# A transformer trunk on one core: x fetched in halves, the root spread later, the memory tokens later

## The chip, the core and the metric

The kernel runs on one core of a Trainium2 chip. Its engines work side by side and wait for each other through semaphores: PE (TensorE, matrix products and transposes), PEld (PE's weight loads), DVE (VectorE), ACT (ScalarE), POOL (GpSimd) and SP (SyncE, which here only issues transfers). The metric is the device time of one execution in microseconds, median of several runs. A difference of less than about 0.3% (1.1 us here) can't be told from no change, since three runs of one kernel lie that far apart.

## The reference, cut to what matters

One layer on x of 256 tokens and 1024 features, all in float32: a mixer of four attention groups of four heads (dilated, stick-breaking, sliding window, block-sparse), a cross-attention into 256 memory tokens, and a squared-ReLU MLP, each with a residual, then a last RMSNorm.

```python
for l in range(DEPTH):
    x = x + hybrid_mixer(rmsnorm(x, g_mix[l]), w_in[l], g_group[l], sinks[l], w_out[l], rel_table)
    x = x + memory_cross_attention(rmsnorm(x, g_cross[l]), rmsnorm(mem, g_mem[l]),
                                   w_xq[l], w_xkv[l], w_xo[l])
    x = x + squared_relu_mlp(rmsnorm(x, g_mlp[l]), w_up[l], w_down[l])
return rmsnorm(x, g_final)
```

## The kernel before, in words

**The products.** Tokens are handled in two blocks of 128 rows, t = 0 and 1. A float32 product is made of three products of float32r parts (high with high, high with low, low with high), `mm3`. So each operand is split: ACT writes the high part (`w<-raw` on L313, `hThi<-tmp` on L396), DVE the rest as the low part (`w<-raw,w` on L314, `hTlo<-tmp,hThi` on L397). Weights come in halves of 512 KB (tile `raw`, four buffers, issued by SP on L299): a fifth half can be issued only when the first half's low part is made.

**The head of the program.** Both blocks of x are fetched (L328), their sums of squares taken on ACT (`sq<-x`, L388), and they are transposed on PE (L403), multiplied by the gain on DVE (`tmp<-ps,gT`, L413) and split into hT. The gain itself is transposed on PE (L374) and copied by ACT (`gT<-ps`, L375). Warm-up products of zeros (`warm`, L365) fill PE before. Then come the projections of the first group: av (48 products on L491), aq and ak (48 each on L420 to L422), then bq and bk. I write av0, av1 and so on for the halves of a weight unit.

**The reciprocal root.** DVE makes the variance (L382), POOL raises it to the power -0.5 (`rstd`, L383), PE transposes the two results (L455, "spread"), ACT copies them to `rk` and `rq` (L458, L459), and DVE multiplies q and k by them when their products are complete (L506).

**The bias.** PE makes a strip by distance (L467), DVE adds its mask (`k<-ps,k`, L468), POOL writes it to DRAM (`dstrip`, L469) and fetches it back in Toeplitz layout, 512 KB for each of three groups and 128 KB for one (L709), on POOL's own queue.

**What sets the order.** Operations are recorded with what they read and write and a price. `Plan.arrange` is a list schedule over the engines: of the operations that can start when an engine gets free, it takes the one with the longest way to the end. Each engine then runs its instructions strictly in that order, so that a wait of one holds up all behind it on its engine. A `raw` or `w` buffer is taken in the order of the recording.

Of the kernel before, what the change touches and what calls it, by code (L numbers as in the profile page):

```python
# [18 lines left out]
P = 128  # L19
S = 256  # L20
D = 1024
# [21 lines left out]
def _constants():  # L43
    """One-hot of minus the bucket of each distance, and the additive mask of each bias row.
    Column u stands for the distance u - 127. Rows 0-3 dilated, 4-7 window, 8-11 causal, 12 strictly past."""
# [17 lines left out]
class Buf:  # L63
    """A tile that is taken from its pool when the first operation on it is issued."""
# [21 lines left out]
class Plan:  # L86
    """Records operations with what they read and write, and issues them in the order of a list schedule:
    of the operations that can start when an engine gets free, the one with the longest way to the end."""
# [126 lines left out]
def trunk(ctx: ExitStack, tc: tile.TileContext, a: dict, out: bass.AP):  # L215
# [24 lines left out]
    def copy(n, out_, in_, r, w):  # L240
        """A copy out of PSUM, by whichever engine is free first."""
        plan.add("DVE", 0.065 + n * 1.05e-3, lambda: nc.vector.tensor_copy(out_(), in_()), r, w,
                 ("ACT", 0.02 + n * 0.00093, lambda: nc.scalar.activation(out_(), in_(), AF.Copy)))
# [10 lines left out]
    def dma_late(nbytes, fn, r, w):  # L254
        """On the queue of GpSimd."""
        plan.add("POOL", 1.0, fn, r, w)
        plan.add("DMA", max(0.06, nbytes / 360e3), None, [], w)
# [34 lines left out]
    def load(u, *which):  # L292
        """Fetches and splits halves of a unit."""
# [23 lines left out]
    def wt(u, k):  # L317
        """Row block k of a unit: the two buffers and the block's place in them."""
        got, n = parts[u]
        return got[k // n], k % n  # L320

# [5 lines left out]
    def load_x(t):  # L327
        dma(P * D * 4, lambda: nc.sync.dma_start(xt[t].t, a["x"][0, tsl(t), :]), [], [xt[t]])  # L328
# [9 lines left out]
    load_x(0)  # L338
    load_gain(0, nc.scalar)
    load("av", 0)  # L340
    load_x(1)
    load("av", 1)
    ident, mhalf, warm = buf("ident", [P, P]), buf("mhalf", [P, 1]), buf("warm", [P, 512], BF16)
    pool(0.5, lambda: make_identity(nc, ident.t), [], [ident])
    pool(0.05, lambda: nc.gpsimd.memset(mhalf.t, -0.5), [], [mhalf])
    dve(512, lambda: nc.vector.memset(warm.t, 0.0), [], [warm])
# [13 lines left out]
    def warm_up(n):  # L360
        """Products of nothing, so that the array's clock is up when the first ones come."""
        wps = acct()
        plan.fixed = -1.0
        for _ in range(n):
            pe(0.11, lambda: nc.tensor.matmul(wps[:, 0:P], warm[:, 0:P], warm[:, 0:P], start=True, stop=True), [warm], [wps])  # L365
# [5 lines left out]
    def gains_T(i):  # L371
        n = grow[i].shape[0]
        gps = pst()
# [6 lines left out]
    def rstd_of(ssq, n):  # L380
        v, r = buf("var", [P, 1], F32, 4), buf("rstd", [P, 1], F32, 16)
        dve(1, lambda: nc.vector.tensor_scalar(v.t, ssq.t, 1.0 / n, EPS, op0=ALU.mult, op1=ALU.add), [ssq], [v])  # L382
        pool(0.5, lambda: nc.gpsimd.tensor_tensor(r.t, v.t, mhalf.t, op=ALU.pow), [v, mhalf], [r])  # L383
        return r

    def rstd_row(src, view, n):
        sq, ssq = buf("sq", [P, D], BF16, 1), buf("ssq", [P, 1], F32, 4)
        act(n, lambda: nc.scalar.activation(sq[:, 0:n], view(), AF.Square, accum_out=ssq.t), [src], [sq, ssq], 1)  # L388
        return rstd_of(ssq, n)
# [9 lines left out]
    def transpose(dst, src, view, n, keys):  # L399
        """n blocks of 128 columns of view(), transposed side by side into dst."""  # L400
# [5 lines left out]
    def gained_T(x, g, hl, t):  # L406
        """The transposed rows of x, times the gain, split: (t, half of the blocks) at a time."""
# [21 lines left out]
    def proj_T(dst, view, u, i, hT):  # L429
        """view()[c, t] = sum_k w[k, c] hT[k, t]"""  # L430
# [5 lines left out]
    def proj(dst, view, u, hT, t):  # L436
        """view()[t, c] = sum_k hT[k, t] w[k, c]"""
# [6 lines left out]
    h1 = pair("hT", KB, 2)  # L444
    r1 = []
    for t in range(2):
        gained_T(xt[t], 0, h1, t)
        r1.append(rstd_row(xt[t], lambda t=t: xt[t].t, D))
# [77 lines left out]
    def transpose_probs(w, t):  # L526
        """w [t, 4, s] -> per head the blocks [s, t], each with its buffer."""
# [15 lines left out]
    def weigh(pT, v, kv, vkeys):  # L543
        """Weighted values and their sums: [t, 4, 65]."""
# [26 lines left out]
    # ---- scores of 128 queries and 256 keys by float32r products: a head's two parts of k above each other in the  # L571
    #      rows of the array, met by the high part of q twice; then the low part of q with the high part of k ----
# [3 lines left out]
    def stack_k(k, view, n):  # L576
        """Slot 2 i + half: the high part of the head's rows, and in the other rows their low part."""
# [8 lines left out]
    def stack_q(q, view):  # L586
        """The high part twice, above each other, and the low part in its own rows."""
# [107 lines left out]
    def rows_mm(acc, hl, u, t, c0, c1, first, last):  # L695
        """acc += columns c0 to c1 of the sum over the two row blocks of a unit"""
# [19 lines left out]
    for gi in range(4):  # L716
# [3 lines left out]
        if gi == 1:  # L720
            mem = [buf("tmp", [P, D], F32, 3) for _ in range(2)]
            for t in range(2):
                dma(P * D * 4, lambda t=t: nc.sync.dma_start(mem[t].t, a["mem"][0, tsl(t), :]), [], [mem[t]])
# [93 lines left out]
    def up_rows(i, hid, t):  # L817
        """Two blocks of hidden features for one block of tokens alone."""
# [107 lines left out]
```

## Time and profile before

| | |
|---|---|
| median of 3 runs | 361.29 us (360.21 to 361.37) |
| span of the profiled execution, first to last instruction | 357.2 us |
| median less span (launch and end, outside the span) | 4.1 us |
| PE busy | 347.0 us, 97% of the span |
| DVE, ACT, POOL busy | 230.7, 194.1, 24.9 us |
| DMA | 59.88 MB, 168 GB/s over the span |

The time of the profiled execution is known by its span alone; sums are made against 357.2 us, and the 4.1 us around it are taken as constant. PE's busy time counts a product until its modelled end, so 97% says that PE rarely has nothing in flight, not that it is at its peak.

### The profile page before, as it was taken

The page shows a single profiled execution, that of the slowest core. Times are in us where ns is not written, and L with a number is a line of the kernel's source. Part 1 is how long each engine was busy: PE and PEld are TensorE (multiplying, and loading weights), DVE is VectorE, ACT ScalarE, POOL GpSimd, SP SyncE. Part 2 cuts the span into 40 slices and gives each one's busy share as a digit, 9 for nine tenths or more (in the row PEclk, how much of TensorE's full clock was granted, in tenths as well). Part 3 has the DMA queues.
Part 4 walks back from the last instruction along what each step waited for, and adds up shares of the span by engine and source line. Part 5 has one row for each costly group of instructions (what it writes and reads, how often), then busy time and mean ns, then how long its engine had stood idle before and what let it go on. Part 6 is the DMA issues. An engine that isn't in the chain of part 4 may idle for free.

```text
span 357.2 us, 6139 instructions
## 1 busy us (share of the span) xinstructions
PE 347.0 (97%) x2442; PEld 316.9 (89%) x2442; DVE 230.7 (65%) x370; ACT 194.1 (54%) x313; POOL 24.9 (7%) x44
## 2 busy tenths in 40 slices
PE   7899999999999999999999999999999999999992
PEld 6798999989888889878999999999999999999982
DVE  3857779579886699668946445464555545465254
ACT  6577677377873467684654435354353534535132
POOL 5430100000201005000010000000000000000000
PEclk9999999999999999999999999999999999999998
DMA  8998574640245335825375555655466554653003
GB/s 247 357 348 254 140 217 124 229 119 0 65 167 182 120 118 159 260 65 167 103 252 178 176 163 192 219 181 192 137 218 195 185 200 135 229 190 107 2 0 117
DMA packets 39900, 59.88 MB, mean 168 GB/s; under 512 B 2006, under 2 KB 33040, under 8 KB 39872
## 3 DMA queue, kind: packets, MB, share of 16 engines
q1 hardware_dynamic: 39216, 57.69, 50.3%
q0 software_dynamic: 640, 1.80, 1.7%
q8 instruction: 19, 0.31, 0.3%
q14 instruction: 9, 0.07, 0.1%
q10 hardware_dynamic: 16, 0.00, 0.0%
HBM read 58.42 MB, written 1.07 MB: 167 GB/s over the span
## 4 chain that ended last, share of the span: by engine, by line
PE 91%; DVE 2%; issue 2%; DMA 2%; POOL 1%; ACT 0%; SPq 0%; POOLq 0%; DVEq 0%
PE acc L420 15%; PE acc L421 15%; PE acc L422 15%; PE ps L421 11%; PE ps L420 11%; PE ps L422 11%; PE ps L553 4%; PE ps L403 3%; PE ps L601 2%; PE ps L600 2%; PE ps L535 2%; DMA x<-in_x_dram 2%; POOL rstd L383 1%; PE ps L629 1%; DVE hTlo L397 1%
## 5 line engine op out<-in xcount | busy, mean ns | idle before, releaser
L314 DVE TENSOR_TENSOR w<-raw,w 128x1024 fp32r<-128x1024 f32 x100 | 120.3, 1220 | 83.4 <-ACT w L313 80.0
L313 ACT ACTIVATE w<-raw 128x1024 fp32r<-128x1024 f32 x100 | 103.4, 1054 | 93.7 <-PE ps L421 43.5
L421 PE MATMUL ps<-hTlo,w 128*128 128x256 f32 x256 | 72.2, 282 | 0.0
L420 PE MATMUL ps<-hThi,w 128*128 128x256 f32 x256 | 72.0, 281 | 0.0
L422 PE MATMUL ps<-hThi,w 128*128 128x256 f32 x256 | 71.8, 280 | 0.0
L420 PE MATMUL acc<-w,yThi 128*128 128x512 f32 (+1 forms) x168 | 64.1, 381 | 0.0
L421 PE MATMUL acc<-w,yThi 128*128 128x512 f32 (+1 forms) x168 | 63.0, 375 | 0.0
L422 PE MATMUL acc<-w,yTlo 128*128 128x512 f32 (+1 forms) x168 | 62.5, 372 | 0.0
L422 PEld LDWEIGHTS ps<-hThi,w 128*128 128x128 f32 x256 | 48.4, 189 | 0.0
L420 PEld LDWEIGHTS ps<-hThi,w 128*128 128x128 f32 x256 | 48.2, 188 | 0.1
L421 PEld LDWEIGHTS ps<-hTlo,w 128*128 128x128 f32 x256 | 48.1, 188 | 0.1
L422 PEld LDWEIGHTS acc<-w,yTlo 128*128 128x128 f32 x168 | 31.5, 188 | 6.1
L420 PE MATMUL acc<-hThi,w 128*128 128x256 f32 x128 | 36.6, 286 | 0.0
L420 PEld LDWEIGHTS acc<-w,yThi 128*128 128x128 f32 x168 | 31.6, 188 | 5.7
L421 PEld LDWEIGHTS acc<-w,yThi 128*128 128x128 f32 x168 | 31.7, 189 | 5.2
L421 PE MATMUL acc<-hTlo,w 128*128 128x256 f32 x128 | 36.1, 282 | 0.0
L422 PE MATMUL acc<-hThi,w 128*128 128x256 f32 x128 | 36.0, 281 | 0.0
L383 POOL TENSOR_TENSOR rstd<-var,mhalf 128x1 f32<-128x1 f32 x16 | 14.9, 932 | 149.6 <-DVE var L382 102.8
L420 PEld LDWEIGHTS acc<-hThi,w 128*128 128x128 f32 x128 | 24.1, 188 | 0.5
L422 PEld LDWEIGHTS acc<-hThi,w 128*128 128x128 f32 x128 | 24.2, 189 | 0.1
L421 PEld LDWEIGHTS acc<-hTlo,w 128*128 128x128 f32 x128 | 24.1, 188 | 0.0
L830 ACT ACTIVATE q<-ps 128x512 f32<-128x512 f32 x15 | 9.0, 599 | 11.8 <-PE ps L422 11.8
(151 smaller groups left out, 523.6 us busy)
## 6 DMA issues: line engine op xcount, KB each, us to landing
raw<-in_w_up_dram SPq DMA_DIRECT2D x32, 512.0 KB, 3.8
raw<-in_w_down_dram SPq DMA_DIRECT2D x32, 512.0 KB, 3.8
raw<-in_w_in_dram SPq DMA_DIRECT2D x22, 512.0 KB, 4.9
raw<-in_w_out_dram SPq DMA_DIRECT2D x8, 512.0 KB, 3.4
raw<-in_w_xkv_dram SPq DMA_DIRECT2D x4, 512.0 KB, 3.7
w<-dstrip POOLq DMA_DIRECT2D x3, 512.0 KB, 8.3
x<-in_x_dram SPq DMA_DIRECT2D x2, 512.0 KB, 6.0
tmp<-in_mem_dram SPq DMA_DIRECT2D x2, 512.0 KB, 5.8
```

The lines of the kernel that those rows point to most:

```text
L313: act(1024, lambda raw=raw, hi=hi: nc.scalar.activation(hi.t, raw.t, AF.Copy), [raw], [hi])
L314: dve(1024, lambda raw=raw, hi=hi, lo=lo: nc.vector.tensor_sub(lo.t, raw.t, hi.t.bitcast(F32)), [raw, hi], [lo])
L383: pool(0.5, lambda: nc.gpsimd.tensor_tensor(r.t, v.t, mhalf.t, op=ALU.pow), [v, mhalf], [r])
L403: nc.tensor.transpose(dst[:, tsl(k)], view()[:, tsl(k)], ident.t)
L420: nc.tensor.matmul(dst, lh, rh, start=start, stop=False)
L421: nc.tensor.matmul(dst, lh, rl, start=False, stop=False)
L422: nc.tensor.matmul(dst, ll, rh, start=False, stop=stop)
L535: nc.tensor.transpose(pt[:, tsl(i)], w[:, h, tsl(j)], ident.t)
L553: nc.tensor.matmul(view()[:, h, :], z[:, i, :], v[:, j, kv(h), :], start=j == 0, stop=j == len(pT[h]) - 1)
L600: nc.tensor.matmul(dst, qs[:, i, :], ks[:, j, :], start=True, stop=False)
L601: nc.tensor.matmul(dst, ql[own, i // 2, :], ks[own, j, :], start=False, stop=True)
L830: act(512, lambda: nc.scalar.activation(r.t, pu.t.rearrange("p (i t) -> p i t", i=2), AF.Relu), [pu], [r])
```

## The change

The blocks of x are fetched in halves of 512 columns: x's first block by SP and ACT, one half each, the second block by SP in two halves, all ahead of the weight halves av0 and av1 (before: x0, av0, x1, av1). Of the 30 warm-up products the first 10 read a float32r tile of zeros instead of a bfloat16 one. The transposed gains go to a buffer of the ring `acc` instead of `ps`. The price of POOL's power is 3.0 for the two blocks of x and 0.6 elsewhere (before 0.5). The fetch of the memory tokens is recorded as depending on the first group's result for t = 0. Comments are removed; nothing else is changed, but the list schedule gives another order from these inputs. Lines move by up to four: L382 becomes L386, L455 L459, L467 L471, L491 L495, L420 L424, L506 L510.

```diff
-    def load_x(t):
-        dma(P * D * 4, lambda: nc.sync.dma_start(xt[t].t, a["x"][0, tsl(t), :]), [], [xt[t]])
+    def load_x(t, engs):
+
+        for n, eng in enumerate(engs):
+            dma(P * D * 2, lambda n=n, eng=eng: eng.dma_start(xt[t][:, nsl(n)], a["x"][0, tsl(t), nsl(n)]), [], [(xt[t], n)])
...
-    load_x(0)
+    load_x(0, (nc.sync, nc.scalar))
     load_gain(0, nc.scalar)
-    load("av", 0)
-    load_x(1)
-    load("av", 1)
-    ident, mhalf, warm = buf("ident", [P, P]), buf("mhalf", [P, 1]), buf("warm", [P, 512], BF16)
+    load_x(1, (nc.sync, nc.sync))
+    load("av")
+    ident, mhalf, warm = buf("ident", [P, P]), buf("mhalf", [P, 1]), buf("warm", [P, 256], BF16)
+    warm_r = buf("warm_r", [P, P], F32R)
...
-    dve(512, lambda: nc.vector.memset(warm.t, 0.0), [], [warm])
+    dve(128, lambda: nc.vector.memset(warm_r.t.bitcast(F32), 0.0), [], [warm_r])
+    dve(256, lambda: nc.vector.memset(warm.t, 0.0), [], [warm])
...
-        for _ in range(n):
-            pe(0.11, lambda: nc.tensor.matmul(wps[:, 0:P], warm[:, 0:P], warm[:, 0:P], start=True, stop=True), [warm], [wps])
+        for i in range(n):
+            z = warm_r if i < 10 else warm
+            pe(0.11, lambda z=z: nc.tensor.matmul(wps[:, 0:P], z[:, 0:P], z[:, 0:P], start=True, stop=True), [z], [wps])
...
-        gps = pst()
+        gps = acct()
...
-    def rstd_of(ssq, n):
+    def rstd_of(ssq, n, cost):
...
-        pool(0.5, lambda: nc.gpsimd.tensor_tensor(r.t, v.t, mhalf.t, op=ALU.pow), [v, mhalf], [r])
+        pool(cost, lambda: nc.gpsimd.tensor_tensor(r.t, v.t, mhalf.t, op=ALU.pow), [v, mhalf], [r])
...
-    def rstd_row(src, view, n):
+    def rstd_row(src, view, n, cost=0.6):
...
-        r1.append(rstd_row(xt[t], lambda t=t: xt[t].t, D))
+        r1.append(rstd_row(xt[t], lambda t=t: xt[t].t, D, 3.0))
...
-                dma(P * D * 4, lambda t=t: nc.sync.dma_start(mem[t].t, a["mem"][0, tsl(t), :]), [], [mem[t]])
+                dma(P * D * 4, lambda t=t: nc.sync.dma_start(mem[t].t, a["mem"][0, tsl(t), :]), [yT[0][0]], [mem[t]])
```

How the order moves is shown at three places. The first is DVE in the head of the program, before the change: the products with the gain for x's first block, av0's low part, then x's second block.

```order
L413 TENSOR_TENSOR tmp_143<-ps_127,gT_0_135 128x512
L382 TENSOR_SCALAR var_157<-ssq_117 128x1
L314 TENSOR_TENSOR w_159<-raw_102,w_149 128x1024
L413 TENSOR_TENSOR tmp_179<-ps_163,gT_0_135 128x512
L413 TENSOR_TENSOR tmp_179<-ps_169,gT_0_135 128x512
```

And DVE after the change, behind the four products with the gain, from the last two low parts of hT to the low parts of av0, av1, aq0 and aq1.

```order
L401 TENSOR_TENSOR hTlo_177<-tmp_149,hThi_172 128x4x128
L401 TENSOR_TENSOR hTlo_177<-tmp_162,hThi_172 128x4x128
L472 TENSOR_TENSOR k_103<-ps_185,k_103 13x384
L386 TENSOR_SCALAR var_205<-ssq_124 128x1
L386 TENSOR_SCALAR var_209<-ssq_160 128x1
L314 TENSOR_TENSOR w_213<-raw_135,w_183 128x1024
L314 TENSOR_TENSOR w_230<-raw_165,w_191 128x1024
L314 TENSOR_TENSOR w_245<-raw_179,w_203 128x1024
L314 TENSOR_TENSOR w_260<-raw_188,w_235 128x1024
```

The low part of av0 stood between the two blocks of x and now stands behind all of hT, the bias strip and both variances, and four low parts of weights follow each other.

The second place is PE from the last products of av (L491, now L495) to those of aq and ak. Before, the root's transposes stand ahead of aq:

```order
L491 MATMUL acc_181<-w_238,hThi_155 128x256 x4
L455 MATMUL ps_264<-ident_65,rstd_161 128x128
L455 MATMUL ps_264<-ident_65,rstd_255 128x128
L491 MATMUL acc_195<-w_238,hThi_155 128x256 x3
L420 MATMUL acc_277<-hThi_155,w_214 128x256
```

After the change they stand behind 14 of aq's 16 groups of three products, and 12 products of av for t = 1 follow aq:

```order
L459 MATMUL ps_320<-ident_67,rstd_226 128x128
L459 MATMUL ps_320<-ident_67,rstd_271 128x128
L424 MATMUL acc_262<-hThi_172,w_235 128x256
L425 MATMUL acc_262<-hTlo_177,w_235 128x256
L426 MATMUL acc_262<-hThi_172,w_260 128x256
...
L495 MATMUL acc_207<-w_191,hThi_172 128x256 x4
L495 MATMUL acc_207<-w_191,hTlo_177 128x256 x4
L495 MATMUL acc_207<-w_230,hThi_172 128x256 x4
L424 MATMUL acc_365<-hThi_172,w_336 128x256
```

The third place is DVE around the first group's q and k (L506, now L510). Before, the low parts of ak stand ahead of q, the memory tokens are scaled (L733), and one low part, that of bq0 (`w_424`), stands between q and k:

```order
L314 TENSOR_TENSOR w_345<-raw_221,w_325 128x1024
L314 TENSOR_TENSOR w_362<-raw_294,w_340 128x1024
L506 TENSOR_TENSOR q_376<-acc_277,rq_281 128x512
L733 TENSOR_SCALAR tmp_245<-tmp_245,rstd_352 128x1024
L733 TENSOR_SCALAR tmp_267<-tmp_267,rstd_357 128x1024
L593 TENSOR_TENSOR ql_405<-q_376,qs_390 64x256 x2
L314 TENSOR_TENSOR w_424<-raw_368,w_407 128x1024
L506 TENSOR_TENSOR k_444<-acc_364,rk_275 128x512
```

After:

```order
L510 TENSOR_TENSOR q_340<-acc_262,rq_331 128x512
L314 TENSOR_TENSOR w_357<-raw_249,w_336 128x1024
L314 TENSOR_TENSOR w_362<-raw_266,w_359 128x1024
L597 TENSOR_TENSOR ql_382<-q_340,qs_353 64x256 x2
L314 TENSOR_TENSOR w_398<-raw_288,w_377 128x1024
L314 TENSOR_TENSOR w_411<-raw_302,w_393 128x1024
L314 TENSOR_TENSOR w_433<-raw_387,w_419 128x1024
L510 TENSOR_TENSOR k_449<-acc_365,rk_326 128x512
```

Both low parts of ak (`w_357`, `w_362`) now stand behind q, and those of bq0, bq1 and bk0 (`w_398`, `w_411`, `w_433`) ahead of k. On ACT the copies `rk` and `rq` likewise stand ahead of the high part of ak0 (`w_336`). From the MLP on, all engines have the order that they had.

## Rows read from the trace of the kernel before

**Rows 1.** The page: the span, and busy time of each engine.
```profile
span 357.2 us, 6139 instructions
...
PE 347.0 (97%) x2442; PEld 316.9 (89%) x2442; DVE 230.7 (65%) x370; ACT 194.1 (54%) x313; POOL 24.9 (7%) x44
```
**Rows 2.** PE's longest wait: waiter, releaser: us in total, times, longest.
```profile
PE ps L455 <- POOL rstd L383: 1.3, 1, 1.3
```
**Rows 3.** Windows: stretch, its length, busy us of each engine, PEclk, DMA share, GB/s.
```profile
32.00:90.00 58.00, 58.00 (x467) 54.30 (x466) 46.73 (x109) 38.54 (x79) 1.76 (x4) 1.00 0.46 138
```
**Rows 4.** Timeline 0 to 12: start, us, engine, line, what, [idle before <-releaser].
```profile
1.18 2.74 PE L365 MATMUL acc<-warm 128*128 128x128 bf16 x24 [1.18 <-DVE warm L346]
...
4.17 1.06 ACT L388 ACTIVATE sq<-x 128x1024 bf16<-128x1024 f32 x1 [2.17 <-DMA x<-in_x_dram]
...
4.29 1.08 PE L403 MATMUL ps<-ident,x 128*128 128x128 f32 x4 [0.37 <-DMA x<-in_x_dram]
...
5.61 0.18 ACT L375 ACTIVATE gT<-ps 128x8 f32<-128x8 f32 x1 [0.29 <-PE ps L374]
...
5.82 1.53 DVE L413 TENSOR_TENSOR tmp<-ps,gT 128x512 f32<-128x512 f32 x2 [4.70 <-ACT gT L375]
...
6.63 1.38 ACT L396 ACTIVATE hThi<-tmp 128x512 fp32r<-128x512 f32 x2
...
7.33 1.21 DVE L314 TENSOR_TENSOR w<-raw,w 128x1024 fp32r<-128x1024 f32 x1
...
7.69 1.72 PE L403 MATMUL ps<-ident,x 128*128 128x128 f32 x8 [0.43 <-DMA x<-in_x_dram]
...
9.81 0.81 PE L467 MATMUL ps<-q,rel 32*13 32x384 f32 x2
10.05 2.48 DVE L397 TENSOR_TENSOR hTlo<-tmp,hThi 128x512 fp32r<-128x512 f32 x4
```
**Rows 5.** Timeline 12 to 32, from the bias strip to the first group's q.
```profile
12.46 0.54 DVE L468 TENSOR_TENSOR k<-ps,k 13x384 f32<-13x384 f32 x1
...
12.98 3.47 DVE L314 TENSOR_TENSOR w<-raw,w 128x1024 fp32r<-128x1024 f32 x3
...
13.87 3.04 POOL L383 TENSOR_TENSOR rstd<-var,mhalf 128x1 f32<-128x1 f32 x1
...
16.96 0.32 PE L455 MATMUL ps<-ident,rstd 128*128 128x128 f32 x1 [1.28 <-POOL rstd L383]
...
17.32 0.39 ACT L458 ACTIVATE rk<-ps 128x256 f32<-128x256 f32 x1 [1.18 <-PE ps L455]
...
17.39 0.83 POOL L709 DMA_DIRECT2D w<-dstrip  x1 [0.49 <-DMA dstrip<-k]
...
17.47 0.28 PE L420 MATMUL acc<-hThi,w 128*128 128x256 f32 x1
...
23.13 0.28 PE L420 MATMUL acc<-hThi,w 128*128 128x256 f32 x1
...
23.45 0.68 DVE L506 TENSOR_TENSOR q<-acc,rq 128x512 f32<-128x512 f32 x1
```
**Rows 6.** DVE's and ACT's timelines, 26 to 42: k, and bq1's high part.
```profile
28.98 0.69 DVE L506 TENSOR_TENSOR k<-acc,rk 128x512 f32<-128x512 f32 x1 [0.74 <-PE acc L422]
...
29.13 1.06 ACT L313 ACTIVATE w<-raw 128x1024 fp32r<-128x1024 f32 x1 [2.15 <-PE acc L491]
```
**Rows 7.** The chain that ended last: the first scores from k and q.
```profile
30.13 0.65 PE ps L629 x8
```
**Rows 8.** DMA, 22 to 28: queues (q0 POOL's, q1 SP's) with packets, MB, share; L299's issues of 22.4 and 23.6.
```profile
q0 software_dynamic: 467, 1.67, 81.5%
q1 hardware_dynamic: 426, 0.42, 22.3%
...
DMA to landing us min/median/max: 8.5/8.5/8.5
```
**Rows 9.** DVE's timeline, 50 to 100: the idle time before 70.
```profile
70.09 2.36 DVE L314 TENSOR_TENSOR w<-raw,w 128x1024 fp32r<-128x1024 f32 x2 [4.39 <-ACT w L313]
```

More of the change, by code (lines that the diff above doesn't have):

```diff
@@ L377, in trunk @@
     gains_T(0)
-    def rstd_of(ssq, n):
+    def rstd_of(ssq, n, cost):
         v, r = buf("var", [P, 1], F32, 4), buf("rstd", [P, 1], F32, 16)
         dve(1, lambda: nc.vector.tensor_scalar(v.t, ssq.t, 1.0 / n, EPS, op0=ALU.mult, op1=ALU.add), [ssq], [v])
-        pool(0.5, lambda: nc.gpsimd.tensor_tensor(r.t, v.t, mhalf.t, op=ALU.pow), [v, mhalf], [r])
+        pool(cost, lambda: nc.gpsimd.tensor_tensor(r.t, v.t, mhalf.t, op=ALU.pow), [v, mhalf], [r])
         return r
-    def rstd_row(src, view, n):
+    def rstd_row(src, view, n, cost=0.6):
         sq, ssq = buf("sq", [P, D], BF16, 1), buf("ssq", [P, 1], F32, 4)
         act(n, lambda: nc.scalar.activation(sq[:, 0:n], view(), AF.Square, accum_out=ssq.t), [src], [sq, ssq], 1)
-        return rstd_of(ssq, n)
+        return rstd_of(ssq, n, cost)
     def pair(tag, n, bufs):
```

## The prediction

> **What bounds the kernel now.** First the page: PE is busy 347.0 of 357.2 us [rows 1]. Then its waits: the longest is 1.3 us, for the root on POOL [rows 2]. Then the windows: from 32 to 90 PE is busy 58.00 of 58.00 at the granted clock 1.00, that is 2.4 GHz [rows 3]. So PE's stream is the bound from about 17 us on. A change of order there wins nothing; it can only open a gap, and a gap is paid in full. Only the head can give time back, and there DVE and ACT are as full as PE, so I follow all three [rows 4, 5]: when does PE start aq (17.47 before), and does it run on from there?
>
> In the head before, x's second block lands late (PE transposes it at 7.69), DVE uses the gap for av0's low part at 7.33, and PE has nearly all of av done when it stops 1.28 us ahead of the second transposed root at 16.96 [rows 4, 5].
>
> **Prices.** One product of 256 columns: (23.13 - 17.47)/48 = 0.118 us [rows 5]. On DVE a gain product (5.82 + 1.53 for two) 0.76, and 0.70 is taken as the two at most overlap; four low parts of hT 2.48; bias strip 0.54; a weight's low part 3.47/3 = 1.16 in a stream, 1.21 alone. On ACT a square 1.06, hThi 1.38/2 = 0.69, a weight's high part 1.06 [rows 4, 5, 6]. On PE in the head, four transposes 1.72/2 = 0.86 and a warm-up product 2.74/24 = 0.114 [rows 4].
>
> **The change part by part.**
>
> *x in halves from two queues.* Before, 512 KB from one queue lands for a first use at 4.17 [rows 4]. Two halves from two queues are the same bytes; I take 4.2 for both. Bounds: 3.4 if the second queue doubled the rate (half of the 1.5 us that 512 KB take below), 5.0 if x1's first half, issued by SP right behind, took an equal share. The Trainium skill says in "DMA: Bandwidth & Descriptors", section "Issuing engines are not separate DMA queues", that transfers of all issuing engines run on the same 16 DMA engines, so that several queues save issue time alone; by that rule too x0 lands at about 4.2. No row here shows x on two queues; the other bound would take 0.8 us off the first term below. x1 now lands before av0, some 2 us sooner than at 7.69.
>
> *The head's chain.* The gain's copy `gT` came 1.32 us after the first transposes (5.61 - 4.29). Now one more group of four transposes (0.86) and two warm-up products (0.23) stand ahead of it on PE: gT at 4.2 + 1.32 + 1.09 = 6.6 and the first gain product at 6.8 instead of 5.82 [rows 4]. DVE then runs without a hole: gains to 9.6, low parts of hT to 12.1, bias strip to 12.65, two variances to 12.9 (an estimate: 128x1 elements each), and the low parts of av0, av1, aq0, aq1 at 14.05, 15.2, 16.4, 17.55. ACT: gT and x1's square to 7.95, four hThi to 10.7, high part of av0 at about 11.65. So x1's early arrival is eaten: hT is done 0.4 us sooner than before (10.05 + 2.48 = 12.53), but av0's low part, which the gap at 7.33 had hidden, is now 1.2 us of the chain.
>
> PE: av's 16 products with av0's high part 11.65 to 13.55; av0's low part at 14.05; then 20 products to about 16.45; aq's low part is there at 16.4. aq starts at 16.45, its end with the two root transposes (0.3) is 22.4, and the 12 products of av left behind end at 23.8. Before, all this was done at 23.13, but for one product (0.12). The gains' second transposes (0.1) are moved in from later. First term: 23.8 - 23.25 - 0.1 = **+0.45**. The 1.28 of the root's wait is gone, but wait for the weights' low parts has taken its place.
>
> *The root later.* PE reaches the root's transposes after 14 groups, 16.45 + 14 x 0.354 = 21.4. As before, ACT's `rk` starts 0.36 after the second transpose (16.96, 17.32): 21.9, `rq` ends at 22.65, and only then comes ak0's high part, to 23.7. DVE waits for aq's end and rq with q (22.7 to 23.4), then ak0's low part takes 23.75 to 24.95. PE comes for it at 23.8 + 2 x 0.118 = 24.04 and waits. Before, both low parts of ak were ready ahead of q. Second term: **+0.9**. ak's second half needs its low part at 26.4, when it is ready. Bounds of the term: nothing, if q and rq come 0.9 sooner relative to PE, 1.2 if DVE is late with q.
>
> *k behind bk0.* Before, k was ready at 28.98 + 0.69 = 29.67 [rows 6], ahead of PE, which made the first scores at 30.13 [rows 7]. DVE now makes k after the low part of bk0. That half's `raw` buffer is free when ak0's low part is made, so its fetch is issued at 24.95. There the Toeplitz reads are in the way: from 22 to 28 POOL's queue moved 1.67 MB and SP's 0.42, and a half issued at 23.6 took 8.5 us to land, at 32.1 [rows 8]. It had bk0 and the rest of bq1 ahead of it; bq1's split began at 29.13 [rows 6], so one half per 1.5 us, and the first one through at about 29.0. After the change bk0 is the first in line, but the Toeplitz reads move too: POOL's power ran 3.04 us beside DVE's stream of low parts and ended 0.46 after it (16.91 and 16.45) [rows 5]. The stream now ends at 17.55, so the first root comes at 18.0, the second some 0.5 later, and the first Toeplitz issue at 18.5 instead of 17.39: 1.1 later. bk0 lands at 30.1, its high part is made at 31.15, the low part at 32.4, k (0.69 [rows 6]) at 33.1, and the first scores stand behind k. PE would be there after ak (23.8 + 0.9 + 5.66 = 30.4) and five groups of three (1.77), at 32.2. Third term: **+0.95**. Bounds: nothing, if bk0 lands by 29 (the line of the Toeplitz reads shared evenly); 2.0, if it lands as the half of 23.6 did, 8.5 us after its issue.
>
> *Memory tokens later.* Their two squares leave ACT, their scaling leaves DVE in the head; they come back around 65 to 70, where DVE is idle for 4.39 us [rows 9]. No cost; without that cover some 1.4 us. They also leave SP's queue to bq, which no longer waits for the Toeplitz reads; that is in the third term.
>
> *Warm-up in float32r.* Ten products. Lower bound 0.114 each, as the others; upper bound by the plain float32 products of L467: 0.81 us for two of 384 columns [rows 4], so 0.27 for 128 columns, and twice that, 0.54, as the array goes at half its later pace here (0.114 for 128 columns, later 0.118 for 256 [rows 4, 5]). The later float32r products are no slower for their type, so I take the lower one; all 20 end by 3.5, ahead of x.
>
> Sum: 0.45 + 0.9 + 0.95 = **2.3**. 357.2 + 2.3 + the 4.1 between span and median = **363.6 us**. PE's stream behind it is full before and after, so nothing there gives it back.
>
> **The rivals.**
> *Faster: the root's wait goes and nothing takes its place.* For it: PE's only long wait of the head is removed [rows 2], and x1 comes earlier. Against: ACT and DVE stand behind the same transposes, and the orders give ak0's low part after q. It decides at ak0: its low part must be ready when PE has done av, at 24.0, and k at 32. Price -1.28: 357.2 - 1.3 + 4.1 = 360.0. Chance 0.14.
> *Much the same: only part of the terms comes.* x0 lands at 3.4 and takes 0.8 off the first term, bk0 gets its share of the DMA engines and the third is nothing; the wait for ak0 stays: -0.35 + 0.9 = +0.55, 361.9. For it: SP's share in [rows 8] is not zero. Against: the half issued there took 8.5 us. Chance 0.26.
> *Slower still: the ten float32r products last 5.4 us.* Then the array is free at 1.2 + 5.4 + 1.1 = 7.7, not at 4.2, and DVE's and ACT's chains start 3.5 later: 363.6 + 3.5 = 367.1 at most, 365 if they last half of that. Against: the pace of aq's float32r products [rows 5]. Chance 0.1.
>
> The forecast, all three terms within their bounds, has 0.5.
>
> **How the numbers follow.** The likeliest gives 363.6, from 362.5 to 365 by itself. Over 0.3% is 1.1 us, about what a measurement of this kernel can tell. Slower takes the forecast and the last rival, 0.60; same 0.26; faster 0.14. The range reaches over the same case to 360.4, and up to 365.5, which leaves out the last rival's far end and the faster one's core: some 0.2.
>
> **What would show it.** Right: gT's copy near 6.6, aq's first product near 16.4, the root's transposes without a wait near 21.4; a wait of PE in the third product of ak near 24 for a low part; DVE idle ahead of bk0's low part, k near 33, and scores right behind it. Wrong: gT before 5.8, ak running through, bk0 landing before 29, or k ready before PE comes for it. From the MLP on the times of a stretch should be as before.

## The result and the profile after

The changed kernel took 364.24 us (median of 17 runs, 361.60 to 366.00) beside 361.72 us (median of 17, 359.09 to 366.66) for the kernel before: ratio 1.0059, 95% interval 1.0037 to 1.0082, so about 2.1 us slower. Medians and ranges here take all runs, while ratios leave out the slow ones, over 1.5% above the fastest of their kernel. Runs of one kernel differ by 2 us and more with the clock that TensorE was granted, so I compare kernels at like mean clock as well: where it was 0.995 or more, the median is 359.21 before (17 runs, all from beside the experiments below) and 362.23 after (5 runs), 3.0 us more. The mean counts falls of the clock, not the stretch before its first rise: it is 0.995 in the profile of before, where the clock first rises at 9.0 us.

The page of the profiled execution, to be set against [rows 1]: span 5.3 us longer, which takes in two falls of the clock, and PE as full as before.

```profile
span 362.5 us, 6140 instructions
...
PE 350.6 (97%) x2442; PEld 322.1 (89%) x2442; DVE 232.0 (64%) x372; ACT 193.4 (53%) x312; POOL 25.3 (7%) x44
```

PE's waits after the change (waiter, releaser, us in total, times, longest). The wait for the root [rows 2] is gone; there are one for av0's high part, two for low parts of weights and one for k.

```profile
PE acc L495 <- ACT w L313: 2.6, 1, 2.6
PE acc L369 <- DVE warm_r L348: 1.0, 1, 1.0
PE acc L426 <- DVE w L314: 0.9, 2, 0.6
PE ps L407 <- DMA x<-in_x_dram: 0.4, 1, 0.4
PE ps L633 <- DVE k L510: 0.2, 1, 0.2
```

Windows of the same execution: stretch, length, busy us of PE, PEld, DVE, ACT, POOL, then PEclk, DMA share, GB/s.

```profile
9.00:12.00 3.00, 0.45 (x3) 0.45 (x4) 2.98 (x7) 3.00 (x5) 0.00 (x0) 1.00 1.03 340
12.00:16.00 4.00, 4.00 (x22) 3.73 (x21) 3.49 (x5) 2.39 (x4) 3.72 (x3) 0.57 0.50 120
...
36.00:90.00 54.00, 54.00 (x436) 51.07 (x435) 43.36 (x101) 36.39 (x77) 2.92 (x5) 1.00 0.48 155
...
100.00:108.00 8.00, 7.96 (x40) 6.34 (x38) 5.49 (x16) 5.22 (x11) 1.34 (x1) 0.79 0.27 79
```

From 9 to 12 PE is busy for 0.45 us, while DVE and ACT have no hole. Behind that the granted clock falls: 0.57 on average from 12 to 16, that is 1.2 GHz for 3.4 us of it, and again 0.79 from 100 to 108. The second fall alone costs 1.6 us: the 300 products and transposes of PE that start from 88.1 on take 50.5 us here, and 48.9 in the run with 50 warm-up products below, where the clock held. From 36 to 90 PE is as full as before [rows 3]. The timeline, where it answers to [rows 4, 5, 6]:

```profile
1.04 2.40 PE L369 MATMUL acc<-warm_r 128*128 128x128 f32 x10 [1.04 <-DVE warm_r L348]
4.15 1.06 ACT L392 ACTIVATE sq<-x 128x1024 bf16<-128x1024 f32 x1 [2.14 <-DMA x<-in_x_dram]
...
6.41 2.48 DVE L417 TENSOR_TENSOR tmp<-ps,gT 128x512 f32<-128x512 f32 x4 [5.28 <-ACT gT L379]
7.25 0.66 PE L407 MATMUL ps<-ident,x 128*128 128x128 f32 x4 [0.38 <-DMA x<-in_x_dram]
11.55 0.74 PE L495 MATMUL acc<-w,hThi 128*128 128x256 f32 x4 [2.62 <-ACT w L313]
12.02 3.47 DVE L314 TENSOR_TENSOR w<-raw,w 128x1024 fp32r<-128x1024 f32 x3
16.43 0.83 POOL L713 DMA_DIRECT2D w<-dstrip  x1
17.75 0.28 PE L424 MATMUL acc<-hThi,w 128*128 128x256 f32 x1
17.79 1.50 POOL L713 DMA_DIRECT2D w<-dstrip  x2
...
23.21 0.39 ACT L462 ACTIVATE rk<-ps 128x256 f32<-128x256 f32 x1 [5.20 <-PE ps L459]
23.75 1.06 ACT L313 ACTIVATE w<-raw 128x1024 fp32r<-128x1024 f32 x1
24.00 0.69 DVE L510 TENSOR_TENSOR q<-acc,rq 128x512 f32<-128x512 f32 x1 [6.44 <-PE acc L426]
24.85 2.49 DVE L314 TENSOR_TENSOR w<-raw,w 128x1024 fp32r<-128x1024 f32 x2 [0.17 <-ACT w L313]
25.17 0.28 PE L424 MATMUL acc<-hThi,w 128*128 128x256 f32 x1
25.29 0.28 PE L425 MATMUL acc<-hTlo,w 128*128 128x256 f32 x1
26.11 4.39 SPq L299 DMA_DIRECT2D raw<-in_w_in_dram  x3
26.13 0.39 PE L426 MATMUL acc<-hThi,w 128*128 128x256 f32 x1 [0.57 <-DVE w L314]
31.54 1.06 ACT L313 ACTIVATE w<-raw 128x1024 fp32r<-128x1024 f32 x1 [1.58 <-DMA raw<-in_w_in_dram]
32.63 1.23 DVE L314 TENSOR_TENSOR w<-raw,w 128x1024 fp32r<-128x1024 f32 x1 [1.39 <-ACT w L313]
33.31 0.28 PE L425 MATMUL acc<-hTlo,w 128*128 128x256 f32 x1
33.77 0.68 DVE L510 TENSOR_TENSOR k<-acc,rk 128x512 f32<-128x512 f32 x1
33.91 0.39 PE L426 MATMUL acc<-hThi,w 128*128 128x256 f32 x1 [0.32 <-DVE w L314]
34.51 0.72 PE L633 MATMUL ps<-k,q 64*128 64x128 f32 x8 [0.21 <-DVE k L510]
```

Three places are to be seen. At 11.55 PE has stood still for 2.62 us. At 26.13 the third product of ak starts 0.84 us behind the second instead of 0.12: the low part of ak0 is late because ACT made rk and rq ahead of ak0's high part (23.21, 23.75) and DVE made q ahead of its low part (24.00, 24.85); a stall of 0.72. At 33.91 and 34.51 the products around the first scores start 0.60 apart each, a stall of 0.48 each: bk0's high part was begun when the half landed, at 31.54, its low part at 32.63, and k behind that at 33.77.

### The profile page after: what moved, and what is told of

The parts are those of the page before. It is cut to its first block, busy times and chain, and to the rows that moved or that the text cites. A ratio compares the mean times of both kernels' runs of the same rounds, so it can differ in the third digit from the quotient of the medians.

```text
span 362.5 us, 6140 instructions
## 1 busy us (share of the span) xinstructions
PE 350.6 (97%) x2442; PEld 322.1 (89%) x2442; DVE 232.0 (64%) x372; ACT 193.4 (53%) x312; POOL 25.3 (7%) x44
## 4 chain that ended last, share of the span: by engine, by line
PE 87%; ACT 5%; DMA 3%; issue 2%; DVE 1%; POOLq 0%; POOL 0%; SPq 0%; DVEq 0%; ACTq 0%
PE acc L424 14%; PE acc L425 14%; PE acc L426 14%; PE ps L424 11%; PE ps L426 10%; PE ps L425 10%; PE ps L557 3%; PE ps L407 2%; PE ps L539 2%; PE ps L605 2%; PE acc L495 2%; PE ps L604 2%; DMA raw<-in_w_in_dram 1%; ACT w L313 1%; DMA x<-in_x_dram 1%
## 5 line engine op out<-in xcount | busy, mean ns | idle before, releaser
L424 PE MATMUL ps<-hThi,w 128*128 128x256 f32 x256 | 72.7, 284 | 0.0
L424 PE MATMUL acc<-w,yThi 128*128 128x512 f32 (+1 forms) x168 | 63.8, 380 | 0.0
L425 PEld LDWEIGHTS ps<-hTlo,w 128*128 128x128 f32 x256 | 49.1, 192 | 0.1
L424 PEld LDWEIGHTS ps<-hThi,w 128*128 128x128 f32 x256 | 49.1, 192 | 0.1
L426 PEld LDWEIGHTS ps<-hThi,w 128*128 128x128 f32 x256 | 49.1, 192 | 0.0
L426 PE MATMUL acc<-hThi,w 128*128 128x256 f32 x128 | 36.4, 284 | 0.9 <-DVE w L314 0.9
L424 PE MATMUL acc<-hThi,w 128*128 128x256 f32 x128 | 37.2, 291 | 0.0
L424 PEld LDWEIGHTS acc<-w,yThi 128*128 128x128 f32 x168 | 31.9, 190 | 4.8
L424 PEld LDWEIGHTS acc<-hThi,w 128*128 128x128 f32 x128 | 24.5, 191 | 0.6
L387 POOL TENSOR_TENSOR rstd<-var,mhalf 128x1 f32<-128x1 f32 x16 | 13.8, 864 | 152.5 <-DVE var L386 125.9
```

Source lines behind the costliest of these rows:

```text
L387: pool(cost, lambda: nc.gpsimd.tensor_tensor(r.t, v.t, mhalf.t, op=ALU.pow), [v, mhalf], [r])
L424: nc.tensor.matmul(dst, lh, rh, start=start, stop=False)
L425: nc.tensor.matmul(dst, lh, rl, start=False, stop=False)
L426: nc.tensor.matmul(dst, ll, rh, start=False, stop=stop)
```

## The experiments

Each edit keeps every other instruction in place, unless said otherwise. `plan.moves` takes one operation out of the finished order and puts it directly ahead of another, or behind it with "after"; ("lo", "bk", 0) is the low part of bk0, "ak" is the multiplication that makes k, "aq" the one that makes q. In these kernels lines lie up to 25 further down. The experiments ran on three chips, each beside runs of the kernel before on that chip; the changed kernel was not run again there, so a difference of medians against its 364.24 is only a rough guide. The intervals of its edited versions all overlap with its own, so a verdict on a single edit rests on its trace.

**The hole ahead of av, and the clock.**

```diff
-WARM = 30
+WARM = 50
```

> After the change with 50 warm-up products instead of 30; 18 more of them stand on PE ahead of the bias strip, where PE was idle from 8.93 to 11.55 before av's first product. No other engine's order changes. Theory 1 (the clock): the granted clock fell to 0.50 at 12.22 because PE had stood still for 2.6 us; with the hole filled it stays at 1.00, aq starts at 16.4 to 16.5 as predicted instead of 17.75, and the time falls by 1.3 us, to 362.9 (ratio to before 1.003). Theory 2 (the chain on ACT and DVE sets aq's start whatever the clock): aq starts no sooner than 17.5, the time stays at 364.2. Theory 3 (given back): aq starts 1.3 sooner, but bk0 lands when the Toeplitz reads let it, PE waits that much longer ahead of the scores, and the time stays within 0.3 of 364.2.

363.99 us (362.05 to 364.40), ratio to before 1.0061 (1.0029 to 1.0093). PE's waits in its profile, and behind them the window from 12 to 16:

```profile
PE acc L426 <- DVE w L314: 1.3, 2, 0.8
...
PE acc L495 <- ACT w L313: 1.0, 1, 1.0
```
```profile
12.00:16.00 4.00, 3.37 (x29) 3.17 (x28) 4.00 (x6) 2.14 (x3) 3.70 (x2) 1.00 0.49 144
```

The clock stayed at 1.00, aq started at 16.22 and ak at 23.62, 1.5 us sooner than in the changed kernel's profile. But the scores came at 33.67, only 0.84 sooner, because the wait for bk0's low part grew (0.8 us now), and the median is the same. By the median theory 3 holds; by the two profiles about half of the 1.5 is given back at bk0. At a mean clock of 0.995 and more the changed kernel (362.23) and this one (362.24, 4 runs) agree, but that says little of the fall: it takes 0.005 off the mean, so the runs of 0.996 and more (4 of 17 of the changed kernel) had none.

**ak's parts ahead of rk, rq and q.**

```diff
+    plan.moves.append((('hi', 'ak', 0), 'rk'))
+    plan.moves.append((('hi', 'ak', 1), 'rk'))
+    plan.moves.append((('lo', 'ak', 0), 'aq'))
+    plan.moves.append((('lo', 'ak', 1), 'aq'))
```

> After the change with one move: ACT makes both high parts of ak ahead of rk and rq, DVE both low parts ahead of q, as before the change; PE, POOL and SP keep their order. Theory 1 (the second term is the order on ACT and DVE): PE's stall of 0.73 us in the third product of ak goes. With ak's low parts made near 19 to 22, bk0's fetch is issued 4 to 6 us sooner than 26.1, so that bk0 lands before k's product is complete at 31.5 and most of the third term (0.96) goes too: -1.7 us, 362.5. Theory 2 (the line of the Toeplitz reads starves SP's queue whenever the fetch is issued): bk0 lands at 31 or later, k still waits, only 0.7 us goes: 363.5. Theory 3 (another wait takes its place, for instance bq0 or q): less than 0.3 us goes.

363.92 us (362.13 to 366.04), ratio 1.0076 (1.0042 to 1.0110). SP's transfers and ACT's high parts of bk0 in its profile:

```profile
20.72 10.44 SPq L308 DMA_DIRECT2D raw<-in_w_in_dram  x4
...
31.25 1.06 ACT L322 ACTIVATE w<-raw 128x1024 fp32r<-128x1024 f32 x1 [1.93 <-DMA raw<-in_w_in_dram]
```

The stall in ak is gone, so the second term's cause is the order on ACT and DVE. No time came of it: bk0's fetch is issued at 20.72 instead of 26.11, yet the half lands at 31.25 instead of 31.54, and PE still stalls for 0.53 and 0.48 us in front of the scores. That is theory 2; its gain of 0.7 can't be seen in the median, nor at like clock (362.60, 3 runs).

**k ahead of bk0's low part.**

```diff
+    plan.moves.append(('ak', ('lo', 'bk', 0)))
```

> After the change with one move: DVE makes the first group's k ahead of bk0's low part; nothing else moves on any engine. Theory 1 (the third term is k standing behind bk0): k starts when its last product is complete, near 31.9, instead of 33.77; the first scores start without PE's two stalls of 0.48 us each, and 0.96 us goes: 363.3. Theory 2 (bk0's low part is late next): PE waits for bk0 instead, in the products of bk behind the first scores, and at most 0.3 us goes: 364.

363.81 us (361.68 to 364.27), ratio 1.0043 (1.0010 to 1.0076). DVE and PE in its timeline:

```profile
30.44 0.69 DVE L522 TENSOR_TENSOR k<-acc,rk 128x512 f32<-128x512 f32 x1 [0.71 <-PE acc L436]
...
33.01 0.39 PE L436 MATMUL acc<-hThi,w 128*128 128x256 f32 x1 [0.76 <-DVE w L323]
```

k is made 3.3 us sooner and no longer holds the scores. But a product of bk0 stands ahead of them on PE, and it waits for the same low part. In the run with 50 warm-up products, whose clock held as it does here, the scores came at 33.67, here at 33.33. At like clock (361.78, 3 runs) the median is 0.45 us lower, which runs this few can't tell from nothing. The third term has two causes, k behind the low part on DVE and bk0's first product ahead of the scores on PE; both wait for one transfer.

**The three together.** The edits above in one kernel.

> After the change with all three edits of the runs above: 50 warm-up products, ak's high and low parts ahead of rk, rq and q, and k ahead of bk0's low part. Theory 1 (three separate losses that add up): -1.3 - 0.73 - 0.96 = -3.0 us, 361.2, a little below the kernel before (361.7). Theory 2 (they cover each other; one wait behind them all, for a transfer, sets the time): the gain is no more than that of the best single edit, 362.5 to 363.

363.26 us (361.30 to 363.99), ratio 1.0046 (1.0015 to 1.0077). One row of ACT tells why the gains don't add up:

```profile
30.72 1.06 ACT L322 ACTIVATE w<-raw 128x1024 fp32r<-128x1024 f32 x1 [3.22 <-DMA raw<-in_w_in_dram]
```

bk0's fetch was issued at 20.14 here and landed at 30.7, as in the run with k ahead, where ACT's row stands at 30.64. PE waits 0.7 and 0.8 us for its two parts. Theory 2: the three losses stand in front of one transfer.

**The Toeplitz reads behind k.** POOL reads an element of k ahead of the reads of groups 2 and 3; they keep their order. In the first version the element goes to a new tile of 4 bytes per partition (`mhalf2`), in the second to `rel`, which is no longer needed; each version has one of the two lines, and moves that put the reads behind k in POOL's order.

```diff
         def go():
+            if gi == 2:
+                nc.gpsimd.tensor_copy(mhalf2.t, late[0].t[:, 0, 0:1])   # first
+                nc.gpsimd.tensor_copy(rel.t[:, 0:1], late[0].t[0:32, 0, 0:1])   # second
             src = dstrip.t
```

> After the change with one edit: POOL reads one element of the first group's k before it issues the Toeplitz reads of groups 2 and 3, so that 1 MB of them starts behind k instead of at 18 us. PE, DVE, ACT and SP keep their order. Theory 1 (the Toeplitz reads set when bk0 lands): bk0, issued near 26, lands within 3 us of its issue, before 29; PE no longer waits in front of the first scores (0.92 and 0.48 us in the run with k ahead, 0.48 and 0.48 in the changed kernel), k is made when its product is complete, and the time falls by 1.0 to 1.4 us, to about 363. Theory 2 (SP's own line of halves sets it): bk0 lands at 30.5 or later again, and the time stays. Theory 3 (the moved reads hold back later halves, behind k, by as much): the waits in front of the scores go, new ones of the same size come between 34 and 45.

> The changed kernel with the Toeplitz reads of groups 2 and 3 behind k, as in the earlier run, but POOL's one element goes to a tile that is there already, not to a new one of 4 bytes, so that no later tile lies elsewhere in memory. Theory 1 (in the earlier run each product of the MLP took 1.1 ns longer on average, 147.52 against 146.42 ns, because the new tile moved the others): the pace is back at 146.4, no wait of 0.4 us or more stands between ak and 50, and the time is 1.0 to 1.4 us below the changed kernel, median near 363. Theory 2 (the moved reads or the extra operation change the pace): 147.5 again, median near 364.

First 363.94 us (363.16 to 365.75), ratio 1.0078 (1.0049 to 1.0107). Second 362.25 us (361.17 to 363.76), ratio 1.0041 (1.0015 to 1.0067). In the second one's profile SP, ACT and DVE, and then all waits of PE that are listed for the whole program:

```profile
25.86 4.39 SPq L309 DMA_DIRECT2D raw<-in_w_in_dram  x3
...
27.55 3.07 ACT L323 ACTIVATE w<-raw 128x1024 fp32r<-128x1024 f32 x3
32.04 0.68 DVE L525 TENSOR_TENSOR k<-acc,rk 128x512 f32<-128x512 f32 x1
```
```profile
PE acc L510 <- ACT w L323: 1.7, 1, 1.7
PE acc L380 <- DVE warm_r L359: 1.0, 1, 1.0
PE acc L437 <- DVE w L324: 0.6, 1, 0.6
```

POOL issues the two reads at 33.28, not at 17.79. bk0's fetch is issued at 25.86, at the same place as after the change, and its high part is made in one run with those of bq0 and bq1 (three without a hole, 27.55 to 30.62): the third begins at 29.6, so the half had landed by then instead of at 31.5. The waits in front of the scores are gone, and the stall in ak alone is left. So the Toeplitz reads of groups 2 and 3, which nothing needs before those groups, are what makes bk0 late. No new wait came behind k; by the trace theory 1. The two profiles are alike in the head (aq at 17.51 here, 17.75 after the change); whether PE would wait for k where the clock holds and aq starts at 16.2 isn't shown. The time doesn't settle it: the first version's is a miss, and the second's is 2.0 us below the changed kernel by the medians and 0.65 by the ratios, whose intervals overlap.

The two versions differ by the place of one written element; PE's instructions and their order are the same. From PE's start times over 800 products of the MLP one product took 147.52 ns on average in the first and 146.42 in the second, as after the change; the groups of 512 columns between 200 and 320 us show it (first version, then second; the mean of one in ns is the last number ahead of the idle time):

```profile
L436 PE MATMUL acc<-w,yThi 128*128 128x512 f32 x62 | 24.6, 396 | 0.0
```
```profile
L436 PE MATMUL acc<-w,yThi 128*128 128x512 f32 x61 | 23.9, 391 | 0.0
```

Over the whole stretch from aq's start to the end of the span that is 343.8 us against 342.3.

**PE's order behind ak as before the change.** k ahead of bk0's low part, and bk0's first product behind the first scores and eight groups of bq:

```diff
+    plan.moves.append(('ak', ('lo', 'bk', 0)))
+    plan.moves.append((('mm', 'bk', 0, 0), ('mm', 'bk', 0, 1)))
+    plan.moves.append((('mm', 'bq', 0, 4), ('mm', 'bk', 0, 0)))
...
```

> After the change with two moves: k ahead of bk0's low part on DVE, and on PE the first scores and eight groups of bq's products ahead of bk0's first product, as before the change. Theory 1 (the third loss is the order alone: PE asks for bk0 ahead of the scores, and bk0 lands at 30.7 at the earliest): no wait of PE between ak's end and 34 us is over 0.2 us, and the time falls by 1.4 us against the changed kernel at the same granted clock (362.1 at 0.996, so 360.7 there), median near 362.8. Theory 2 (PE only comes sooner to the next wait, for bk0 or bq1): a wait of 0.9 or more stands behind the scores, and at most 0.5 us goes.

363.99 us (362.21 to 366.51), ratio 1.0091 (1.0061 to 1.0122). No wait is left between ak and 45 us, but the first group's softmax and its transposes now come behind products that stood later, and PE waits there:

```profile
50.35 0.44 PE L418 MATMUL ps<-ident,yn 128*128 128x128 f32 x2 [0.61 <-DVE yn L704]
```

With one for pT at 45.7 the two cost 0.77 and 0.41 us, as much as was won (0.48 + 0.48). In this profile the clock was at 0.50 from 10.7 to 17.5 and aq started at 18.95, so PE also came to bk0 later than it does where the clock holds. A miss: the stalls that the order removed were bought with others.

**All causes at once.** 50 warm-up products, ak's parts, k, the Toeplitz reads (first version, with the new tile), and the second gains' transpose behind eight groups of aq.

> After the change with all that the runs point to: 50 warm-up products, ak's parts ahead of rk, rq and q, k ahead of bk0's low part, the Toeplitz reads of groups 2 and 3 behind k, and the second gains' transpose (PE waited 0.5 to 0.7 us for its DMA ahead of av's second half) behind eight groups of aq. Theory 1 (head 0.3, ak 0.73, bk0 and k 1.4 to 1.7 make the whole loss of 2.85 at an undisturbed clock, and each cause is met): PE runs from aq's start to the scores without a wait over 0.3 us, aq starts at 15.8 to 16.1, and the time is 359 to 359.5 at a granted clock of 0.996, as the kernel before has it there, median 361 to 361.7. Theory 2 (something else in the changed kernel costs as well): 1 us or more above before at the same clock.

362.78 us (361.90 to 363.66), ratio 1.0044 (1.0020 to 1.0068); at like clock 362.04 (5 runs). From aq on one stall of 0.40 us is left, ahead of the scores, with a listed wait of 0.2. It comes from one of the edits: DVE, idle from 30.5, makes k at 31.26, when its product is complete, and bk0's low part only behind it, at 31.86. The new tile costs its 1.1 ns a product here too (147.52), some 1.6 us by the pair of runs above; without that it would stand near 360.4 at like clock, 1.2 above before. It was not run without the tile, so that number is worked out. 0.4 of the 1.2 is the stall, and 0.3 the head, if that costs here what it does in the runs where the clock held; where the rest is stays open, so neither theory is settled.

**The kernel before with the root later.** The root's transposes 12 groups of aq later, rk and rq behind ak's high parts, the Toeplitz reads behind k; DVE's order is as before, with ak's low parts ahead of q. First with the new tile, then with `rel`.

```diff
+    plan.moves.append(('spread', ('after', ('mm', 'aq', 1, 3))))
+    plan.moves.append(('rk', ('after', ('hi', 'ak', 1))))
+    plan.moves.append(('rq', ('after', 'rk')))
```

> The kernel before with two edits: on PE the root's transposes 12 groups of aq later, on ACT rk and rq behind ak's high parts, and the Toeplitz reads of groups 2 and 3 behind k. DVE keeps its order, with ak's low parts ahead of q. Theory 1 (the root's wait of 1.28 us is real time, if what stands behind the root is not ahead of ak's parts and no transfer binds next): PE starts aq near 16.2 and keeps most of it, at least 0.8 us less than before at the same granted clock (359.0 at 0.995, so 358 there). Theory 2 (PE then waits for bq1's low part or for q as long): within 0.3 us of before.

> The kernel before with the root's transposes 12 groups of aq later and the Toeplitz reads of groups 2 and 3 behind k, as in the earlier run, without the new tile of 4 bytes. Theory 1 (there the tile's place took 1.3 ns off each product of the MLP, 145.12 against 146.43 ns, some 1.2 us in all, and the order took the rest of 2.2): the pace is 146.4, and the time is 0.8 to 1.1 us below before, ratio 0.997. Theory 2 (the pace comes with the moved reads): 145.1 again, ratio 0.991 to 0.994.

With the tile 360.73 us (356.58 to 365.20), ratio 0.9914 (0.9870 to 0.9958); with `rel` 362.51 us (358.29 to 366.88), ratio 1.0014 (0.9970 to 1.0058). The pace of the MLP is 145.12 ns with the tile and 146.43 without, as before, with PE's instructions and their order the same in both. So in this layout the tile takes 1.3 ns off each product, 1.8 us from aq's start to the end (339.3 and 341.1), and the order alone is within the noise of before. The ratios lie 3.6 us apart; what the tile's pace leaves of that stays open. Neither profile shows a wait of PE over 0.2 us behind the head. In both the clock first rose at 16.0 and 16.5 us: with the tile PE's products of 256 columns start 0.21 us apart until then and 0.12 behind, the lower and the higher of the clock's two levels. So aq started later than before, at 19.3.

**The same with the float32r warm-up, and that alone.**

```diff
-            pe(0.11, lambda: nc.tensor.matmul(wps[:, 0:P], warm[:, 0:P], warm[:, 0:P], start=True, stop=True), [warm], [wps])
+            z = warm_r if i < 10 else warm
+            pe(0.11, lambda z=z: nc.tensor.matmul(wps[:, 0:P], z[:, 0:P], z[:, 0:P], start=True, stop=True), [z], [wps])
```

> The kernel before with the root's transposes 12 groups of aq later, the Toeplitz reads of groups 2 and 3 behind k, the tile of 4 bytes, and the first ten warm-up products in float32r from the change. Theory 1 (the float32r products only bring the clock up sooner): granted clock 1.00 from about 5.4 instead of 9.0, PE's work before aq shorter, time the same or up to 0.5 us below the run without them (360.7 median, 357.0 undisturbed), since ACT and DVE set aq's start. Theory 2 (the clock then falls again in the head, as in the changed kernel, where PE idles): a stretch at 0.50 between 12 and 17 us, time 0.5 to 1.5 us above that run.

> The kernel before with one part of the change: the first ten of 30 warm-up products in float32r. All other instructions keep their order. Theory 1 (the fifth term: no cost, all 20 products ahead of x end before x lands): time within 0.5 us of before. Theory 2 (they bring the clock up sooner, at 5.4 as in the changed kernel's profile instead of 9.0): transposes and av's first products are quicker, but aq waits for the root at POOL as before; time within 0.5 us of before too, with the granted clock 1.00 from about 5.4. Theory 3 (they hold PE up): PE's first transpose of x later than 4.4, time above before by as much.

Together with the root later and the new tile 357.05 us (355.38 to 361.84), ratio 0.9900 (0.9866 to 0.9933), the fastest of all. Alone 360.26 us (359.17 to 365.93), ratio 0.9998 (0.9965 to 1.0031). So the warm-up does nothing that can be measured by itself (in its profile the clock rose at 11.7, not at 5.4, and aq started at 18.35), and beside the tile's 0.9914 the 0.9900 is no different. In the fastest one's profile aq starts 1.8 us sooner than at 17.47 [rows 5], and PE's waits are its start, 0.7 for x and 0.2 or less behind. Its span is 3.8 us shorter than that of before: 1.8 of it ahead of aq, and 2.0 from there on, nearly all of which is the tile's pace (1.8). The granted clock first rose at 7.0 there, sooner than the 9.0 of before, so how much of the 1.8 ahead of aq is the order and how much the clock isn't settled:

```profile
15.71 0.28 PE L434 MATMUL acc<-hThi,w 128*128 128x256 f32 x1
```
```profile
PE acc L379 <- DVE warm_r L358: 1.0, 1, 1.0
PE ps L417 <- DMA x<-in_x_dram: 0.7, 1, 0.7
```

## Why the prediction was right

**The total.** 363.6 was forecast, 364.24 measured; a loss of 2.3 us forecast, and 2.1 by the ratio, 2.5 by the medians, 3.0 at like clock measured. One step of the total was loose: device time lies about 2.0 us above the span in the runs that list both (364.53 and 362.5 here), so the profiled execution of before was one of some 359.2 us, a quick one, and only half of the 4.1 between span and median was launch and end. That the terms below missed by some tenths of a us each, to both sides, and still add up, is luck in part.

**The head, +0.45.** Right where the clock held. In the runs with 50 warm-up products and with k ahead, aq started at 16.22 and 16.26 (forecast 16.45) and ak at 23.62 and 23.66 (forecast 23.8), which against 23.25 and a product of 0.1 makes 0.3. The first gain product came at 6.41 (forecast 6.8), av's first at 11.55 (forecast 11.65; its own terms, 10.7 and 1.06, add up to 11.76). x0 was there at 4.15, as [rows 4] had it at 4.17: two queues brought nothing, as the Trainium skill says in "DMA: Bandwidth & Descriptors", section "Issuing engines are not separate DMA queues". x1's first half was transposed at 6.16, but its second at 7.25, not some 2 us sooner than 7.69; it cost nothing, since DVE was the chain. Not foreseen was the hole of 2.62 us on PE, though it follows from the forecast's own numbers, nor the fall of the clock to 1.2 GHz behind it, which put aq at 17.75 in the profiled execution. That the hole causes the fall isn't shown: four runs of the same kernel had none. The run with the hole filled has the same median, while in the profiles 0.84 of its 1.5 us is still there at the scores.

**The root later, +0.9.** Right in place and cause, a little smaller: the third product of ak waits for ak0's low part, 0.72, and the stall goes when ak's parts are put first. The root's transposes themselves didn't wait.

**k behind bk0, +0.95.** Right in size in the profiled execution (0.48 + 0.48), wrong by half in its cause: the forecast had PE wait for k alone, and PE waits for bk0 itself in a product ahead of the scores. That the size came out is luck: without the two stalls PE would have been at the scores at 33.55 (forecast 32.2), since the clock had fallen, and k was ready at 34.45 (forecast 33.1), since bk0 landed at 31.5 and not at 30.1; both are 1.35 late. The step that bk0 is held by the Toeplitz reads is shown by the runs that move them (landed by 29.6) and by those that fetch it 5 to 6 us sooner and still have it near 31. Before the change it landed hardly sooner: by the order of the buffers bk0 is the half issued at 22.4, and 8.5 us on is 30.9 [rows 8]. What is new is that k and the scores stand behind it. Wrong was that the Toeplitz reads would start 1.1 us later; they started at 16.43, 1.0 sooner than at 17.39 [rows 5], and at 17.5 to 17.9 in the profiles of the first four experiments. Where the clock holds in the head, the term is larger than forecast: stalls of 0.92, 0.48 and 0.17, 1.57 in all, in the run with 50 warm-up products. With 0.3 and 0.73 that makes 2.6 of the 2.9 us by which its span (360.1) exceeds that of before.

**Memory tokens, nothing.** PE is busy for 54.00 of 54.00 us from 36 to 90, where their work now lies; not tried by itself.

**Warm-up in float32r, nothing.** Right in effect: ratio 0.9998 alone. The price was off: ten took 2.40 us, 0.22 us from start to start, between the two bounds, and they still end, at 3.44, before x is there.

**The rivals.** The faster one failed where it was to be decided, at ak0 and at the scores. The one with only part of the terms failed on bk0. The slower one failed on the price of the float32r products.

## What to carry to other kernels

A wait removed from the bounding engine is worth only what the next wait behind it leaves: ask which transfer lands last for that engine, and which traffic nobody needs yet stands in front of it; five kernels with edits of order or warm-up in front of bk0 moved the median by 1 us at most, though each took a stall or a hole out of its trace. When an operation is moved on one engine, look at what it pushes back on the others: here rk, rq and q took the place of weight parts that PE wanted sooner. Compare kernels at like granted clock, and test a small edit also against the placement of tiles in memory before its gain or loss is believed.

## What the runs showed of the hardware

**A tile of 4 bytes changed the pace of every product of the MLP**, by +1.1 ns in one kernel (146.42 to 147.52 ns) and by -1.3 ns in the other (146.43 to 145.12), with PE's instructions and their order the same: 1.6 us more and 1.8 us less from aq's start to the end, more than any term here. That it shifts the tiles behind it in memory is inferred. The Trainium skill says in "SBUF — State Buffer", section "Specifications (TRN2)", that memory lines are of 16 bytes and each cross to a new line pays a penalty; that would fit, but no run here shows that it is this.

**A queue can be starved, and issuing sooner didn't help.** bk0 issued at 20.1, 20.7, 24.6 or 26.1 landed at 30.7, 31.25, 30.7 and 31.5 beside POOL's Toeplitz reads; without 1 MB of them it took under 3.8 us (25.86 to 29.6). [rows 8] show how: from 22 to 28 the two queues moved nearly as many packets (467 and 426), but POOL's held 3.6 KB each and SP's 1.0 KB (worked out from the MB), so that POOL's had 80% of the bytes. The Trainium skill says in "DMA: Bandwidth & Descriptors", section "Queues, rings and completion order", that a DMA engine takes turns between queues packet by packet; those counts agree, if the packets of the profile are those of the page. Larger packets for the weights were not tried.

**The granted clock fell where PE had stood still, and also where it had not.** It was at 0.50 for 3.4 us from 12.2 in the profile of the changed kernel, behind a hole of 2.62 us, and not in the run where 1.0 us of the hole was left. But one kernel (k ahead of bk0's low part) kept 1.00 behind a hole of 1.7 us and another (the Toeplitz reads behind k, second version) fell beside one as long, and four runs of the changed kernel itself had no such fall. In four profiles it fell between 100 and 105 with PE busy for nearly all of the stretch before (9.96 of 10.00 us from 90 to 100 in the changed kernel), and in that of the three edits together at 34.5. Its first rise varied as much: 5.4 to 8.3 us in ten profiles with float32r warm-up products and 11.7 in the eleventh, 9.0, 16.0 and 16.5 in the three without. What decides that stays open.
